# A transformer layer's gates' stage: landing buffers of their own for the mixing of the second FFN matrix, and weights asked for two ahead

## The chip, the cores and the metric

One core of a Trainium2 chip runs the whole kernel as one program. The metric is the device time of one execution in microseconds (us); lower is better. Engines are named as the profile names them: PE (TensorE matmul), PEld (its weight loads), DVE (VectorE), ACT (ScalarE), POOL (GpSimd), and SP (SyncE), which here only issues DMAs.

## The reference, cut to what matters

One layer of an encoder: sequence 1024, width 1024, float32. Attention outputs `o_a` (512 wide) and `o_b` (256 wide) are each projected to 1024, weighed by two sigmoid gates of the layer's input, added, projected once more, and followed by a SwiGLU FFN of width 2816.

```python
gate_a, gate_b = jnp.split(jax.nn.sigmoid(gates + b_gate[l]), 2, axis=-1)
merged = gate_a * (o_a @ w_proj_a[l]) + gate_b * (o_b @ w_proj_b[l])
x = x + gt1 * (merged @ w_o[l])

h2 = rms_norm(x, g_norm2[l]) * (1.0 + sc2) + sh2
a, up = jnp.split(h2 @ w_ffn_in[l], 2, axis=-1)
x = x + gt2 * ((jax.nn.silu(a) * up) @ w_ffn_out[l])
```

The second FFN product `@ w_ffn_out` is done at the end of the kernel as a two-by-two block product with seven block multiplications in place of eight; this needs four sums and differences ("mixings") of the blocks of `w_ffn_out`, which are made much earlier, in the stage that this case is about.

## The kernel before, in words

Every float32 operand of a large product is split into a high part (rounded, made by ACT) and a low part (the difference, made by POOL or DVE), and each product takes three matmul passes: high by high, high by low, low by high. A weight tile `raw` of 128x512 lands by DMA (`wload`, a ring of 6 buffers), ACT writes `whi`, and POOL writes `wlo` (`wsplit`, a ring of 10 pairs).

The stages, in order of the program: input projections and attention; the **gates' stage** (PE multiplies the layer's input `hT` with gate weights `in_wg`, ACT takes the sigmoid out of PSUM into `sg`); the **merges** (PE multiplies `oT`, the attention outputs, with `in_wpa` and `in_wpb`; DVE multiplies with the gates and adds; ACT and DVE split the sum into `h2T`); the **wo stage** (the product with `w_o`, token tile by token tile); the FFN's first and second products.

In the gates' stage PE does 21 halves of 24 matmuls each, 128x512: one for the gate (2, 1), then two for each of (3, 0), (3, 1), up to (7, 1). Banks of PSUM for them come in pairs, two of `d` for branch 0 and two of `s` for branch 1, so a half can begin when the sigmoid four halves earlier in this alternation (two halves earlier in its own branch's pair) has been read out. Meanwhile, off PE, two other things are done:

- `o_split`: twelve 128x512 pieces of the attention outputs are read back from `o_d` in DRAM and split into the two tiles `oT0` and `oT1`, which the merges multiply with.
- `w2_combos(k)` for k = 0 to 10: four blocks of `w_ffn_out` (called `in_w` in the profile, as are all weights of the FFN) are loaded, POOL and DVE make two differences each, in place, and four results are stored to `w2_d` (`w_d` in the profile).

The merges are `merge(i)` for i in `MORD` = 3, 4, 5, 6, 7, 2, 0, 1. Beside them `w_o` is brought in: `wo_keep` puts five of its eight row blocks into tiles `wr` that replace gates no longer needed, `wo_slot` puts three into the ring of pairs. `KFIRST` is the order in which the first token tile of the wo stage takes these eight.

PE's order is that of the code. On ACT, DVE, POOL and SP a planner orders the instructions of this part of the program, each engine then runs its list strictly in order, and an instruction that waits holds all behind it on its engine. All DMAs here are issued by SP, and eight counters are used in turn for their ends, so that a DMA is issued only when the eighth before it has landed. Space in SBUF is a stack at each side; a pool that is opened where another was closed waits, tile by tile, for the last use of what lay there.

Of the kernel before, what the change touches and what calls it, by code (L numbers as in the profile page):

```python
# [10 lines left out]
F32 = mybir.dt.float32  # L11
F32R = mybir.dt.float32r
# [3 lines left out]
S = 1024  # L16
# [4 lines left out]
HT = 11  # L21
# [4 lines left out]
LATE = (3, 4, 5, 6, 7)  # L26
MORD = (3, 4, 5, 6, 7, 2, 0, 1)
MSIG = {0: ((2, 0), (2, 1)), 1: ((0, 0), (0, 1)), 2: ((1, 0), (1, 1))}
MKEEP = {3: 3, 4: 4, 5: 5, 6: 6, 7: 7}
MSLOT = {5: 2, 6: 0, 7: 1}  # L30
KFIRST, KLAST, OT = (3, 4, 5, 2, 6, 0, 7, 1), (2, 0, 1, 3, 4, 5, 6, 7), 3
PP, QT, AQ, AT, AV = 100, 0, 0, 0, 0
WARM = 40
XSQ = "avavaaaa"
# [5 lines left out]
def hybrid_layer(ctx: ExitStack, tc: tile.TileContext, x, colp, wada1, wada2, bada2, wqkv, wg, wpa, wpb,  # L40
                 wo, w1, w2, hgain, ropeg, rope, rbias, bmask, g2r, out):
    nc = tc.nc

    def pool(name, side, **kw):
        return tc.alloc_tile_pool(name=name, bufs=1, side=side, reuse_waits="tile", **kw)
# [16 lines left out]
    def bank(tag):  # L62
        return ps.tile([128, 512], F32, tag=tag, name="ps_" + tag)
# [26 lines left out]
    def fview(ap):  # L90
        return ap.bitcast(F32)

    def wload(src, n):
        raw = wp.tile([128, 512], F32, tag="raw", bufs=NRAW, name="raw")
        nc.sync.dma_start(raw[:, :n], src)
        return raw[:, :n]

    def wsplit(r, eng=None):
        n = r.shape[1]
        hi = wp.tile([128, 512], F32R, tag="hi", bufs=NHL, name="whi")  # L100
        lo = wp.tile([128, 512], F32R, tag="lo", bufs=NHL, name="wlo")
        nc.scalar.activation(hi[:, :n], r, AF.Copy)  # L102
        (eng or nc.gpsimd).tensor_sub(lo[:, :n], r, fview(hi[:, :n]))  # L103
        return hi, lo

    def wslot(src, n):
        return wsplit(wload(src, n))
# [27 lines left out]
    def big(name, shape=None, dtype=F32):  # L135
        return ap_.tile(shape or wide, dtype, tag="big", bufs=NBIG, name=name)

    yT = [ap_.tile([128, 4, S], F32, tag="qk", bufs=2, name="yT") for _ in range(2)]
    land = [big("land") for _ in range(NBIG)]
# [433 lines left out]
    def mm_set(pb, wsl, src, ksrc, n, ntot, done, hs):  # L573
        for j in range(n):
            for i, (a, b) in enumerate(PASS):
                nc.tensor.matmul(pb, wsl[a][:, j * 128:(j + 1) * 128], src[b][:, ksrc + j, hs],  # L576
                                 start=(done == 0 and j == 0 and i == 0),
                                 stop=(done + j == ntot - 1 and i == 2))
# [3 lines left out]
    def gate_w(i, br):  # L582
        if (i, br) not in gw:
            gw[i, br] = [wslot(wg[i, :, 8 * br + 4 * j:8 * br + 4 * j + 4, :], 512) for j in range(2)]
# [230 lines left out]
    def sig_tile(i, br):  # L815
        z = sgp.tile(wide, F32, tag="sg", bufs=10, name="sg")
        for hf in range(2):
            sig.setdefault((i, br, hf), z[:, hf * 512:hf * 512 + 512])
# [2 lines left out]
        for br in range(2):  # L821
            sig_tile(i, br)
    sig[2, 1, 1] = sgp.tile([128, 512], F32, name="s2")
    op_ = pool("o", "right")
    oT = [op_.tile([128, 6, S], F32R, name=f"oT{i}") for i in range(2)]

    def gates(i, br):
        gate_w(i, br)
        for hf in range(2):
            hs = slice(hf * 512, hf * 512 + 512)  # L830
            if i * 4 + br * 2 + hf < NPRE:
                continue
            pb = bank("ds"[br])
            for j in range(2):
                mm_set(pb, gw[i, br][j], hT, 4 * j, 4, 8, 4 * j, hs)
            nc.scalar.activation(sig[i, br, hf], pb, AF.Sigmoid, bias=bg_c[:, 8 * br + i:8 * br + i + 1])  # L836

    def sig_load(i, br, hf):
        if i * 4 + br * 2 + hf < NPRE:
            hs = slice(hf * 512, hf * 512 + 512)  # L840
            nc.sync.dma_start(sig[i, br, hf], sig_d[i, br][:, hs])
            nc.scalar.activation(sig[i, br, hf], sig[i, br, hf], AF.Sigmoid)
# [3 lines left out]
    def merge_w(i):  # L846
        if i not in mw:
            mw[i] = wslot(wpa[i], 512), wslot(wpb[i], 256)

    def merge(i):  # L850
        merge_w(i)
        wa, wb = mw[i]
        for hf in range(2):
            hs = slice(hf * 512, hf * 512 + 512)
            ppa, ppb = bank("tv"[hf]), bank("ds"[hf])
            mm_set(ppa, wa, oT, 0, 4, 4, 0, hs)
            mm_set(ppb, wb, oT, 4, 2, 2, 0, hs)
            m, sb = sig[i, 0, hf], sig[i, 1, hf]
            nc.vector.tensor_mul(m, m, ppa)
            nc.vector.tensor_mul(sb, sb, ppb)  # L860
            nc.vector.tensor_add(m, m, sb)
            nc.scalar.activation(h2T[0][:, i, hs], m, AF.Copy)
            nc.vector.tensor_sub(h2T[1][:, i, hs], m, fview(h2T[0][:, i, hs]))

    def o_split():
        for pr in (4, 5, 0, 1, 2, 3):
            for hf in range(2):
                hs = slice(hf * 512, hf * 512 + 512)
                raw = wp.tile([128, 512], F32, tag="raw", bufs=NRAW, name="raw")
                nc.sync.dma_start(raw, o_d[pr][:, hs])  # L870
                hi, lo = oT[0][:, pr, hs], oT[1][:, pr, hs]
                if pr < 4:
                    hi, lo = (z[:, pr].rearrange("p (r w) -> p w r", r=16)[:, 32 * hf:32 * hf + 32] for z in oT)
                    raw = raw.rearrange("p (w r) -> p w r", r=16)
                nc.scalar.activation(hi, raw, AF.Copy)
                (nc.gpsimd if hf else nc.vector).tensor_sub(lo, raw, fview(hi))

    def w2_combos(k):
        b = {}
        for r in range(2):  # L880
            for c in range(2):
                b[r, c] = wload(w2[(k + HT * r) * 128:(k + HT * r + 1) * 128, c * 512:c * 512 + 512], 512)
        t1, t3, t2, t4 = b[0, 0], b[0, 1], b[1, 1], b[1, 0]
        nc.gpsimd.tensor_sub(t1, b[0, 1], b[0, 0])
        nc.vector.tensor_sub(t3, b[1, 1], b[0, 1])
        nc.gpsimd.tensor_sub(t2, b[1, 1], t1)
        nc.vector.tensor_sub(t4, b[1, 0], t2)
        for n, z in enumerate((t1, t2, t3, t4)):
            nc.sync.dma_start(w2_d[n, k], z)

    wow = {}

    def wo_raw(hf, k):
        return wload(wo[k * 128:(k + 1) * 128, hf * 512:hf * 512 + 512], 512)

    def wo_keep(k):

        hi, lo = (sgp.tile(wide, F32R, tag="sg", bufs=10, name="wr") for _ in range(2))
        for hf in range(2):
            hs = slice(hf * 512, hf * 512 + 512)  # L900
            raw = wo_raw(hf, k)
            nc.scalar.activation(hi[:, hs], raw, AF.Copy)
            nc.gpsimd.tensor_sub(lo[:, hs], raw, fview(hi[:, hs]))
            wow[hf, k] = hi[:, hs], lo[:, hs]

    def wo_slot(k):
        for hf in range(2):
            wow[hf, k] = wsplit(wo_raw(hf, k))

    gates(2, 1)  # L910
    n = 0
    for i in LATE:
        for br in range(2):
            gates(i, br)
            if i == 3 and br == 0:
                o_split()
            else:
                w2_combos(n)
                n += 1
    h1l.release()  # L920
    h1p.release()
    h2p = pool("h2", "left")
    h2T = [h2p.tile([128, KT, S], F32R, name=f"h2T{i}") for i in range(2)]

    for n, i in enumerate(MORD):
        merge(i)
        if n == 0:
            w2_combos(9)
            w2_combos(10)
        for z in MSIG.get(n, ()):  # L930
            sig_tile(*z)
            for hf in range(2):
                sig_load(*z, hf)
        if n in MSLOT:
            wo_slot(MSLOT[n])
        if n + 1 < 8:
            merge_w(MORD[n + 1])
        if n in MKEEP:
            wo_keep(MKEEP[n])
    op_.release()  # L940
# [390 lines left out]
```

## Time and profile before

| | us |
|---|---|
| median of 3 runs | 1605.3 (1605.08 to 1607.59) |
| the profiled execution | 1608.76, of which the span of the trace 1607.0 |
| gates' stage and merges, in the span | 635.5 to 832.9 |
| PE busy | 1547.5 (96% of the span) |
| DVE, POOL, ACT busy | 996.6, 694.9, 650.5 |

Times of the trace count from the start of the span. "Busy" for PE has the modelled ends of pipelined matmuls in it, so a 96% busy PE may still lose time; how many matmuls start in a stretch says more. In rows that list instructions, "x" is a count, and what stands in square brackets is the idle time of the engine before it and what ended it. In the table of stretches each engine has its busy time and the number of its instructions, then come the clock that PE was granted (1.00 is full), the mean busy share of the 16 DMA engines, and GB/s.

### The profile page before, as it was taken

How to read it: one execution, taken by the hardware profiler on the slowest of the kernel's cores; microseconds unless marked ns; L12 is line 12 of the kernel's file. 1: busy time of each engine (PE TensorE's matmuls, PEld its weight loads, DVE VectorE, ACT ScalarE, POOL GpSimd, SP SyncE). 2: the span in 40 equal slices, each digit the busy share in tenths (PEclk: the TensorE clock that was granted, in tenths of full speed). 3: DMA queues.
4: the chain of work that ended last, by engine and by line, in shares of the span. 5: the costliest groups of instructions: out<-in, count | busy, mean ns of one | idle time of the engine just before them, and what ended most of it. 6: DMA issues, size and time to landing. Idle time of an engine off the chain costs nothing.

```text
span 1607.0 us, 24545 instructions
## 1 busy us (share of the span) xinstructions
PE 1547.5 (96%) x8240; PEld 1292.7 (80%) x8240; DVE 996.6 (62%) x2162; ACT 650.5 (40%) x1694; POOL 694.9 (43%) x658
## 2 busy tenths in 40 slices
PE   8999999999999999998999996999999999999998
PEld 7888888898888877876778875788888888888886
DVE  6766676766988743322474559866666666435476
ACT  5555555555645453311442223323333333344442
POOL 1432232221101041554362246876676666545566
PEclk9999999999999999999999998999999999999999
DMA  8332231344244352777534111333333333576775
GB/s 338 102 102 78 85 115 47 122 127 133 84 132 129 94 168 68 231 251 243 164 120 178 66 46 40 102 115 105 100 109 100 105 98 120 192 218 193 246 218 171
DMA packets 144446, 219.11 MB, mean 136 GB/s; under 512 B 26800, under 2 KB 64560, under 8 KB 144320
## 3 DMA queue, kind: packets, MB, share of 16 engines
q1 hardware_dynamic: 144320, 217.55, 42.3%
q8 instruction: 65, 1.06, 0.3%
q14 instruction: 61, 0.50, 0.1%
HBM read 163.90 MB, written 53.59 MB: 135 GB/s over the span
## 4 chain that ended last, share of the span: by engine, by line
PE 73%; DVE 9%; DMA 8%; POOL 3%; issue 3%; ACT 3%; SPq 0%; POOLq 0%; DVEq 0%; ACTq 0%
PE ps_d L287 13%; PE ps_t L1071 6%; PE ps_s L1071 6%; PE ps_v L1071 6%; PE ps_d L1071 6%; PE ps_d L598 4%; PE ps_d L1173 3%; PE ps_s L1173 3%; DMA raw<-in_w_dram 2%; PE ps_d L993 2%; PE ps_v L1173 2%; PE ps_t L1173 2%; PE ps_v L576 2%; PE ps_s L438 2%; PE ps_v L479 2%
## 5 line engine op out<-in xcount | busy, mean ns | idle before, releaser
L103 POOL TENSOR_TENSOR wlo<-raw,whi 128x512 fp32r<-128x512 f32 (+2 forms) x245 | 327.3, 1343 | 415.4 <-ACT whi L102 411.0
L102 ACT ACTIVATE whi<-raw 128x512 fp32r<-128x512 f32 (+1 forms) x376 | 218.2, 602 | 382.0 <-DMA raw<-in_wg_dram 71.5
L287 PE MATMUL ps_d<-whi,hT 128*128 128x384 f32 x1152 | 317.1, 343 | 0.5 <-ACT v L322 0.5
L287 PEld LDWEIGHTS ps_d<-whi,hT 128*128 128x128 f32 x1152 | 210.1, 188 | 6.2 <-ACT vs L325 3.5
L103 DVE TENSOR_TENSOR wlo<-raw,whi 128x512 fp32r<-128x512 f32 (+1 forms) x131 | 130.8, 1008 | 103.8 <-ACT whi L102 94.7
L287 PE MATMUL ps_d<-wlo,hT 128*128 128x384 f32 x576 | 193.6, 336 | 0.9 <-POOL wlo L103 0.7
L287 PEld LDWEIGHTS ps_d<-wlo,hT 128*128 128x128 f32 x576 | 108.5, 188 | 1.5 <-POOL wlo L103 1.5
L317 POOL TENSOR_TENSOR ra<-qn,rtab 128x64 f32<-128x64 f32 x48 | 17.1, 357 | 165.8 <-DVE qn L310 125.3
L102 ACT ACTIVATE whi<-ws 128x512 fp32r<-128x512 f32 x60 | 37.9, 632 | 117.0 <-DVE ws L1081 32.1
L1008 POOL TENSOR_TENSOR c<-c 128x512 f32<-128x512 f32 x40 | 63.5, 1588 | 50.2 <-DVE c L1121 42.6
L453 ACT ACTIVATE P<-P,st 128x256 f32<-128x256 f32 (+2 forms) x100 | 46.2, 464 | 69.2 <-DVE st L452 69.1
L1071 PE MATMUL ps_t<-t,whi 128*128 128x512 f32 x160 | 52.0, 406 | 14.4 <-DVE c L1007 12.8
L308 DVE TENSOR_REDUCE ss<-sq 128x4 f32<-128x256 f32 x80 | 33.3, 416 | 45.6 <-ACT sq L305 45.5
L576 PE MATMUL ps_s<-hT,whi 128*128 128x512 f32 x176 | 56.5, 403 | 3.7 <-ACT sg L836 3.7
L453 ACT ACTIVATE P<-P,sx 128x384 f32<-128x384 f32 (+1 forms) x64 | 37.1, 580 | 52.8 <-DVE sx L452 52.8
L464 PE MATMUL ps_t<-ident,P 128*128 128x128 f32 (+1 forms) x336 | 51.8, 275 | 4.7 <-DVE P L456 2.0
L479 PE MATMUL ps_v<-PT,v 128*64 128x128 f32 (+1 forms) x672 | 54.7, 284 | 1.4 <-DVE PT L468 1.4
L598 PE MATMUL ps_d<-hT,whi 128*128 128x512 f32 x176 | 55.5, 397 | 0.0
L1007 DVE TENSOR_TENSOR c<-c 128x512 f32<-128x512 f32 x40 | 46.7, 1169 | 13.9 <-ACT c L1006 13.9
L438 PE MATMUL ps_s<-qk 64*128 64x256 f32 (+3 forms) x492 | 53.7, 321 | 1.6 <-DVE st L452 1.4
L438 PEld LDWEIGHTS ps_s<-qk 64*128 64x128 f32 (+1 forms) x492 | 35.0, 182 | 23.4 <-issue 12.2
L1071 PE MATMUL ps_s<-t,whi 128*128 128x512 f32 x168 | 52.9, 396 | 0.0
(377 smaller groups left out, 3972.8 us busy)
## 6 DMA issues: line engine op xcount, KB each, us to landing
raw<-in_w_dram SPq DMA_DIRECT2D x165, 256.0 KB
ga_d<-c SPq DMA_DIRECT2D x77, 256.0 KB
raw<-ga_d SPq DMA_DIRECT2D x77, 256.0 KB
wa<-in_wada_dram SPq DMA_DIRECT2D x32, 512.0 KB
raw<-in_wqkv_dram SPq DMA_DIRECT2D x80, 192.0 KB
w_d<-raw SPq DMA_DIRECT2D x44, 256.0 KB
raw<-w_d SPq DMA_DIRECT2D x44, 256.0 KB
xt<-in_x_dram SPq DMA_DIRECT2D x16, 512.0 KB
```

Source lines behind the costliest of these rows:

```text
L102: nc.scalar.activation(hi[:, :n], r, AF.Copy)
L103: (eng or nc.gpsimd).tensor_sub(lo[:, :n], r, fview(hi[:, :n]))
L287: nc.tensor.matmul(pd[:, :384], tok(a, k, t), U.w[k][b][:, :384], start=(k == 0 and i == 0), stop=(k == KT - 1 and i == 2))
L438: nc.tensor.matmul(I.pS[h][:nq, :nk], U.qk[a][hs, I.q0:I.q0 + nq], U.qk[2 + b][hs, I.kb0 * 128:I.kb0 * 128 + nk], start=(i == 0), stop=(i ...
L453: nc.scalar.activation(P[:nq, :nk], P[:nq, :nk], AF.Exp, scale=-1.0, bias=nm, accum_out=sm)
L464: nc.tensor.transpose(pt[:, i * 128:i * 128 + nq], P[:nq, i * 128:(i + 1) * 128], ident[:nq, :nq])
L479: nc.tensor.matmul(po[hs, :nq], U.v[:, I.kb0 + i, hs], I.PT[h][:, i, :nq], start=(i == 0), stop=(i == nkb - 1))
L576: nc.tensor.matmul(pb, wsl[a][:, j * 128:(j + 1) * 128], src[b][:, ksrc + j, hs], start=(done == 0 and j == 0 and i == 0), stop=(done + j ...
L598: nc.tensor.matmul(st["p"], gw[i, br][j][a][:, kk * 128:(kk + 1) * 128], hT[b][:, k, hs], start=(k == 0 and q == 0), stop=(k == 7 and q == 2))
L1008: nc.gpsimd.tensor_mul(sg, sg, up) if j not in (0, HT) else nc.vector.tensor_mul(sg, sg, up)
L1071: nc.tensor.matmul(pb, w[p][:, k * 128:(k + 1) * 128], b[q][:, k], start=(k == 0 and i == 0), stop=(k == 3 and i == 2))
L1173: nc.tensor.matmul(pb[m], o[0][a][:, m * 128:(m + 1) * 128], o[1][b], start=(k == 0 and i == 0), stop=(k == HT - 1 and i == 2))
```

## The change: what it does

- `w2_combos` no longer takes its loads from the ring `raw`. It has 22 landing buffers of its own (`l`, 2 KB in each partition), in a pool `land` that lies where `oT` lay and is closed before `oT` is opened.
- So `o_split` moves from the start of the gates' stage to behind the ninth gate (6, 1), and `oT` takes the place of the landing buffers.
- All eleven mixings are spread over the first nine gates (a table `W2C`); two of them stood in the merges before.
- The weights of a gate are asked for two gates ahead, those of a merge two merges ahead.
- `wo_slot` stands one merge earlier each time, with its second half's `wlo` on DVE, and `KFIRST` is reordered to match.

```diff
-MSLOT = {5: 2, 6: 0, 7: 1}
+MSLOT = {4: 2, 5: 0, 6: 1}
+NLAND = 22
+W2C = {0: (0,), 1: (1,), 2: (2, 3), 3: (4,), 4: (5,), 5: (6, 7), 6: (8,), 7: (9,), 8: (10,)}
-KFIRST, KLAST, OT = (3, 4, 5, 2, 6, 0, 7, 1), (2, 0, 1, 3, 4, 5, 6, 7), 3
+KFIRST, KLAST, OT = (3, 4, 2, 0, 5, 6, 1, 7), (2, 0, 1, 3, 4, 5, 6, 7), 3
...
-    op_ = pool("o", "right")
-    oT = [op_.tile([128, 6, S], F32R, name=f"oT{i}") for i in range(2)]
+    lnd = pool("land", "right")
...
-                b[r, c] = wload(w2[(k + HT * r) * 128:(k + HT * r + 1) * 128, c * 512:c * 512 + 512], 512)
+                b[r, c] = lnd.tile([128, 512], F32, tag="l", bufs=NLAND, name="l")
+                nc.sync.dma_start(b[r, c], w2[(k + HT * r) * 128:(k + HT * r + 1) * 128, c * 512:c * 512 + 512])
...
-            wow[hf, k] = wsplit(wo_raw(hf, k))
-
-    gates(2, 1)
-    n = 0
-    for i in LATE:
-        for br in range(2):
-            gates(i, br)
-            if i == 3 and br == 0:
-                o_split()
-            else:
-                w2_combos(n)
-                n += 1
+            wow[hf, k] = wsplit(wo_raw(hf, k), nc.vector if hf else None)
+
+    GS = [(2, 1)] + [(i, br) for i in LATE for br in range(2)]
+    for n, z in enumerate(GS):
+        for y in GS[n:n + 3]:
+            gate_w(*y)
+        gates(*z)
+        for k in W2C.get(n, ()):
+            w2_combos(k)
+        if n == max(W2C):
+            lnd.release()
+            op_ = pool("o", "right")
+            oT = [op_.tile([128, 6, S], F32R, name=f"oT{i}") for i in range(2)]
+            o_split()
...
     for n, i in enumerate(MORD):
+        for z in MORD[n:n + 2]:
+            merge_w(z)
         merge(i)
-        if n == 0:
-            w2_combos(9)
-            w2_combos(10)
...
+        if n + 2 < 8:
+            merge_w(MORD[n + 2])
         if n in MSLOT:
             wo_slot(MSLOT[n])
-        if n + 1 < 8:
-            merge_w(MORD[n + 1])
```

What the planner makes of it is seen in the engines' lists. SP's list before, where the gates' stage begins (`o_d<-stg` and `sig_d<-gsig` are the last stores of the attention stage):

```order
L483 DMA o_d<-stg 128x128
L870 DMA raw<-o_d 128x512 x6
L95 DMA raw<-in_w_dram 128x512 x4
L95 DMA raw<-in_wg_dram 128x512 x2
L889 DMA w_d<-raw 128x512 x2
L95 DMA raw<-in_w_dram 128x512 x2
L889 DMA w_d<-raw 128x512
```

SP's list of the changed kernel at the same place:

```order
L97 DMA raw<-in_wg_dram 128x512
L485 DMA o_d<-stg 128x128
L607 DMA sig_d<-gsig 128x512
L485 DMA o_d<-stg 128x128
L884 DMA l<-in_w_dram 128x512 x9
L891 DMA w_d<-l 128x512
L884 DMA l<-in_w_dram 128x512
L891 DMA w_d<-l 128x512
L884 DMA l<-in_w_dram 128x512 x2
L891 DMA w_d<-l 128x512 x3
```

Nine loads of the second FFN matrix now stand ahead of the first store of a mixing, and no gate weight stands among them: ten of the sixteen loads of gate weights that stood in this stage have moved ahead of it, into the attention stage's part of the list.

SP's list of the changed kernel where the mixings end:

```order
L884 DMA l<-in_w_dram 128x512 x2
L871 DMA raw<-o_d 128x512
L891 DMA w_d<-l 128x512 x3
L871 DMA raw<-o_d 128x512
L891 DMA w_d<-l 128x512
L871 DMA raw<-o_d 128x512
L891 DMA w_d<-l 128x512 x7
L871 DMA raw<-o_d 128x512 x6
L97 DMA raw<-in_wpa_dram 128x512
L97 DMA raw<-in_wpb_dram 128x256
```

The reading back of `o_d`, which stood first in the stage, now surrounds the last stores of the mixings, with the weights of the first merge behind it.

ACT's list before, at the start of the gates' stage (`oT` is the high part of the attention outputs, `sg` and `s` are sigmoids):

```order
L604 ACTIVATE gsig<-ps_d,cp 128x512
L875 ACTIVATE oT_9080<-raw 128x512 x4
L875 ACTIVATE oT_9080<-raw 128x32x16 x2
L836 ACT_TABLE_LOAD
L836 ACTIVATE s_9076<-ps_s,cp 128x512
L875 ACTIVATE oT_9080<-raw 128x32x16 x6
L836 ACTIVATE sg<-ps_d,cp 128x512
```

ACT's list of the changed kernel, from the fourteenth sigmoid of the gates' stage on:

```order
L837 ACTIVATE sg<-ps_d,cp 128x512
L876 ACTIVATE oT_9798<-raw 128x512 x4
L876 ACTIVATE oT_9798<-raw 128x32x16 x2
L837 ACTIVATE sg<-ps_d,cp 128x512
L876 ACTIVATE oT_9798<-raw 128x32x16 x5
L837 ACTIVATE sg<-ps_s,cp 128x512
L876 ACTIVATE oT_9798<-raw 128x32x16
L104 ACTIVATE whi<-raw 128x512
L104 ACTIVATE whi<-raw 128x256
```

The twelve activations into `oT` have moved from ahead of the first sigmoids to between the fourteenth and the seventeenth; the first of them waits for the last stores of the eleven mixings, since `oT` lies in their buffers. Two more merges' weights (`whi`, four rows) follow before the seventeenth sigmoid.

## The prediction

> **What bounds the kernel now.** I read the page's first part for the span, then the stretches of the stage, PE's list of instructions in order of time, and then the lists of the engines that PE waits for. The page:
>
> ```profile
> span 1607.0 us, 24545 instructions
> ```
>
> The stretches (columns: time, then busy time and count of PE, PEld, DVE, ACT and POOL, PE's clock, DMA share, GB/s), first the gates' stage, then the merges, then four pieces:
>
> ```profile
> 635.00:758.00 123.00, 117.76 (x512) 96.31 (x512) 35.08 (x28) 33.43 (x51) 65.13 (x46) 0.97 0.72 239
> 758.00:833.00 75.00, 70.81 (x292) 56.58 (x291) 43.92 (x56) 30.06 (x55) 33.80 (x28) 0.95 0.44 143
> 8.00:12.00 4.00, 3.37 (x31) 3.13 (x30) 2.37 (x8) 2.44 (x7) 0.00 (x0) 1.00 1.03 409
> 659.00:667.00 8.00, 8.00 (x37) 6.60 (x37) 1.61 (x3) 0.64 (x2) 2.97 (x4) 1.00 0.85 284
> 723.00:731.00 8.00, 4.31 (x14) 3.14 (x14) 2.44 (x2) 2.30 (x4) 4.56 (x4) 0.75 0.77 268
> ```
>
> PE is the only engine near full, yet between 723 and 731 it started 14 matmuls where it had started 37 between 659 and 667, at a clock of 0.75. PE's own list gives the pace and the holes:
>
> ```profile
> 635.54 0.74 PE L576 MATMUL ps_s<-hT,whi 128*128 128x512 f32 x2
> ...
> 708.14 0.73 PE L576 MATMUL ps_d<-hT,whi 128*128 128x512 f32 x2 [1.55 <-ACT sg L836]
> ...
> 720.77 0.62 PE L576 MATMUL ps_s<-hT,whi 128*128 128x512 f32 x2
> 721.22 0.39 PE L576 MATMUL ps_s<-hT,wlo 128*128 128x512 f32 x1
> 721.45 0.61 PE L576 MATMUL ps_s<-hT,whi 128*128 128x512 f32 x2
> ...
> 728.70 1.22 PE L576 MATMUL ps_s<-hT,whi 128*128 128x512 f32 x2 [3.69 <-ACT sg L836]
> ...
> 758.42 0.63 PE L576 MATMUL ps_t<-oT,whi 128*128 128x512 f32 x2
> ...
> 765.57 1.22 PE L576 MATMUL ps_d<-oT,whi 128*128 128x512 f32 x2 [4.19 <-ACT sg L836]
> ...
> 832.94 0.87 PE L993 MATMUL ps_d<-wr,h2T 128*128 128x512 f32 x3
> 836.99 6.51 PE L993 MATMUL ps_d<-wr,h2T 128*128 128x512 f32 x15 [3.18 <-DVE sg L860]
> ```
>
> The stage's first matmul starts at 635.54, that of the merges at 758.42, that of the wo stage at 832.94. Undisturbed, three matmuls take 721.45 - 720.77 = 0.68 us, so a half of 24 takes 8 x 0.68 = 5.44 us and the 21 halves 114.2: the gates could end at 749.8 and end at 758.4, 8.6 us late. The merges' undisturbed pace stands in the chain of waits, twelve matmuls in 2.81 us:
>
> ```profile
> 774.06 2.81 PE ps_t L576 x12
> ```
>
> Their 288 matmuls (eight merges, six blocks, two halves, three passes) need 67.5 us and take 74.5, 7.0 late. All of it sits at three holes, 1.55, 3.69 and 4.19 us = 9.4 together; the other 6.2 are mostly matmuls at half clock behind the two longer ones (1.22 us for a pair at 728.70 against 0.62 at 720.77).
>
> All three holes end on a sigmoid `sg`. ACT's list shows what kept it:
>
> ```profile
> 696.84 1.29 ACT L102 ACTIVATE whi<-raw 128x512 fp32r<-128x512 f32 x2 [8.86 <-DMA raw<-in_wg_dram]
> 698.03 0.67 ACT L836 ACTIVATE sg<-ps_s,cp 128x512 f32<-128x512 f32 x1
> ...
> 717.38 1.26 ACT L102 ACTIVATE whi<-raw 128x512 fp32r<-128x512 f32 x2 [8.19 <-DMA raw<-in_wg_dram]
> 718.55 0.67 ACT L836 ACTIVATE sg<-ps_s,cp 128x512 f32<-128x512 f32 x1
> ...
> 727.45 0.63 ACT L102 ACTIVATE whi<-raw 128x512 fp32r<-128x512 f32 x1 [8.23 <-DMA raw<-in_wg_dram]
> 727.98 0.67 ACT L836 ACTIVATE sg<-ps_s,cp 128x512 f32<-128x512 f32 x1
> ```
>
> ACT stands idle 8 to 9 us before a gate weight that has not landed, with sigmoids behind it. The weight is late because SP's list is held. Its waits in 635 to 760, the four of the stores L889:
>
> ```profile
> SPq L889 <- POOL raw L884: 27.1, 10, 4.0
> SPq L889 <- POOL raw L886: 10.5, 11, 1.0
> SPq L889 <- DVE raw L885: 10.2, 11, 2.8
> SPq L889 <- DVE raw L887: 9.3, 10, 1.0
> ```
>
> SP waits 57 us of 125 for mixings whose stores are next in its list, and four of the ring's six buffers hold one mixing, so the next weight cannot be asked for. The DMA share meanwhile is 0.72.
>
> **The change part by part.** *Weights two ahead, and buffers of their own.* Ten of the sixteen gate loads now come before the stage; of the other six the last stands 62nd among its transfers, so at some 0.85 us each (below) lands near 691. It serves the sixteenth half, due at 635.5 + 15 x 5.44 = 717.1: 26 us of cover. The three holes then go, 15.6 us, if nothing takes their place.
>
> *The mixings, squeezed into nine gates.* What is late next is `oT`. All its activations on ACT wait for the last store of a mixing, at a time I call T, and three sigmoids, the 15th to 17th, stand behind them. T is a sum of transfers of 256 KB: 44 loads, 44 stores, 6 gate weights and 6 of the `o_d` loads, 100, behind one another since only eight are in flight. The start comes from SP's list, the latency from the chain:
>
> ```profile
> 636.18 0.38 SPq L483 DMA_DIRECT2D o_d<-stg  x1
> ```
> ```profile
> 660.22 1.91 DMA raw<-in_w_dram
> ```
>
> So the first lands near 636.6 + 1.9 = 638.5 and T = 638.5 + 99 p, where p is the time of one transfer. No row shows these 100 without SP's waits. Bounds: the stage's 239 GB/s at a share of 0.72 make 332 at a full share, p = 262144 B / 332 = 0.79 us, T = 716.7; the 284 GB/s of 659:667 as it stands make 0.92, T = 729.9. Further out, the 409 GB/s of 8:12, reads only, make 0.64, T = 702, and the unchanged 239 make 1.10, T = 747. I take 0.85, between the two nearest: SP's waits shrink but stay in the list. T = 722.7.
>
> DMA and not the engines should set T. The mixing's four operations, and the two for `oT`:
>
> ```profile
> L884 POOL TENSOR_TENSOR raw<-raw x11: 1261/1287/1295, 652.1 to 749.5; 128x512 f32<-128x512 f32 x11
> ```
> ```profile
> L885 DVE TENSOR_TENSOR raw<-raw x11: 691/693/694, 654.0 to 756.2; 128x512 f32<-128x512 f32 x11
> ```
> ```profile
> L886 POOL TENSOR_TENSOR raw<-raw x11: 1262/1292/1297, 656.7 to 757.0; 128x512 f32<-128x512 f32 x11
> ```
> ```profile
> L887 DVE TENSOR_TENSOR raw<-raw x11: 1752/1762/1772, 658.0 to 758.3; 128x512 f32<-128x512 f32 x11
> ```
> ```profile
> L875 ACT ACTIVATE oT<-raw x12: 619/1132/1364, 635.6 to 648.8; 128x512 fp32r<-128x512 f32 x12
> ```
> ```profile
> L876 POOL TENSOR_TENSOR oT<-raw,oT x6: 1303/1924/2528, 636.9 to 650.0; 128x512 fp32r<-128x512 f32 x6
> ```
>
> One after the other they are 1.29 + 0.69 + 1.29 + 1.76 = 5.03 us a mixing, 55.3 for eleven, against 84 us of transfers. POOL has 22 x 1.29 = 28.4 of them and some eleven low parts of weights, differences of the same size and so at the same 1.29, 14, in the same 84.
>
> *What hangs on T.* Behind T come, on the path to the 17th sigmoid: one activation 0.6, six low parts on POOL at 1.92 = 11.5 (the ring's six buffers must come free before the second six can land), about 3 for that second landing, 2.3 for the merges' four weights on ACT (two of 128x512 take 1.29, the other two are half as wide), 0.4 for the last activation, 0.7 for the sigmoid: T + 18.5. The 21st half needs it, at 635.5 + 20 x 5.44 = 744.3. So T may be as late as 725.8 (p = 0.88, 297 GB/s) at no cost, and each us beyond is a us lost. The 15th and 16th sigmoids (T + 5.5 by 733.4, T + 11.8 by 738.9) and the first merge (T + 17 by 749.8) allow more. At 722.7 the margin is 3.1 us: nothing lost.
>
> *Merges and `wo_slot`.* Two mixings leave this stage, eight loads and eight stores at a share of 0.44, so its weights come sooner. Three low parts of 128x512 go from POOL to DVE, about 1 us each by the 0.69 to 1.76 above, under 75 - 43.9 = 31 us of idle DVE. `KFIRST` has the same eight blocks. The first token tile's hole at 836.99 hangs on the last merge's DVE work, which stays: 0, with -6 (hole and half clock gone: 15 matmuls in 6.51 us against 3.4) and +3 (a second such hole) as bounds.
>
> Sum: -8.6 - 7.0 + 0 = -15.6. The profiled execution took 1608.76 (span 1607.0 and 1.76 around it) and would become 1593.2; it lies 3.5 above the median of 1605.3, from which I take the saving: **1589.7**.
>
> **The rivals.** *A: the last store is late.* If p lies between 0.88 and 1.0, the sigmoids behind `oT` open a new hole at the 19th to 21st half. At 0.92, T = 729.9, 4.1 us too late, and a hole like that of 3.69 us brought half clock, worth (3.18-us hole, 6.51 - 3.4) 3.1: the time is 1605.3 - 15.6 + 7.2 = 1596.9; at 1.0 (T = 737.5) 1604.5. For it: no stretch shown moved more than 284 GB/s with loads and stores mixed. Against it: SP waited in every one of them. The Trainium skill, "TensorE: Matmul & The Clock Gate", Part 1, says that the clock halves after about one idle window of some 3.4 us; by it a lateness of 4.1 us dealt to three holes costs no half clock, and A's time would be about 3 us less. The trace agrees as far as the hole of 1.55 us was followed by a pair at 0.73 us; that 3.18 us sufficed shows that the figure is no sharp edge. On p, the Trainium skill, "HBM Reference", Specifications (TRN2), gives about 358 GB/s as a core's share and some 425 for a core alone; an estimate from 358 is T = 711, 15 us ahead of need, which speaks against A. The 409 of 8:12 agree for reads; no row here shows it for stores.
>
> *B: slower than before.* The list's own waits, not the buffers, set the pace: stores wait for POOL in SP's order as before, and 100 transfers go at 239 GB/s. T = 747.1, 21.3 late, with half clock 24.4: 1614.1. It decides from a lateness of 15.6 - 3.1 = 12.5, T = 738.3, p = 1.01 (260 GB/s). For it: the stage never ran far above that pace. Against it: those 57 us of waits came with four loads ahead of their mixing; now nine stand ahead of the first store.
>
> *C: the change does not do what it says.* The sigmoids wait for something that no weight ends, and the holes stay: 1605.3. Against it: three rows of ACT name the weight's DMA, each with a sigmoid close behind.
>
> **How the numbers follow.** My forecast (no hole, p below 0.88) has 0.62, since its bound of 0.88 lies above the middle of the two nearest prices but below the worse; A 0.26, B 0.06, C 0.06. The time of the likeliest is 1589.7. The range reaches down to 1585 (most of the transition's -6) and up to 1600 (A at p = 0.95: T = 732.6, 6.8 late, +9.9), which leaves out B, C and A's slow end, some 0.17. A measurement of this kernel tells about 0.2%, 3.2 us, from no change. Faster by more: the forecast and nearly all of A, 0.86; within: C and A's end, 0.08; slower: B, 0.06. The forecast's own range is 1585 to 1593.
>
> **What the profile after should show.** No hole on `sg` in PE's list before 750, merges starting near 750 and the wo stage near 817; no ACT wait of 8 us on `in_wg`; a DMA share over 0.85 and over 290 GB/s from 640 to T; the last `w_d` store landing at 719 to 726; ACT's first `oT` row right behind it. A is seen as a hole before the 19th to 21st half with ACT's `oT` rows ahead of the sigmoid; B as that hole over 12 us long with SP still waiting on POOL. I would be wrong if a resource that I held hidden carries the end: POOL in the mixings, SP's order between the stores and the `o_d` loads, or the weights of the first merges behind them.

## The result and the profile after

| | before | changed |
|---|---|---|
| median of 4 runs (us) | 1606.44 (1605.08 to 1609.12) | 1589.15 (1587.58 to 1590.5) |
| the profiled execution, its span | 1608.76, 1607.0 | 1587.91, 1586.1 |

The ratio is 0.989 (95% interval 0.9871 to 0.9909): 17.7 us faster, between 14.6 and 20.7. The forecast was 15.6 us faster. Chips differ by some us in the kernel before (medians of 1601.6 to 1607.9 in the experiments below), so kernels are compared by their ratios to the kernel before that ran beside them.

In the changed kernel's chain of waits PE follows on PE from the gates' stage into the wo stage, with no other engine between them:

```profile
637.69 5.71 PE ps_s L578 x24
643.39 10.88 PE ps_d L578 x48
...
741.31 10.88 PE ps_s L578 x48
752.19 2.81 PE ps_t L578 x12
...
818.26 1.41 PE ps_s L578 x6
819.66 11.16 PE ps_d L996 x48
```

Two halves take 10.88 us from the second on, exactly twice 5.44. The stage lasts 114.5 us (637.69 to 752.19) where it lasted 122.9, the merges 67.5 where they lasted 74.5. Among PE's waits there is no row on `sg` in these stages.

The stretches of the changed kernel (columns as before):

```profile
640.00:660.00 20.00, 20.00 (x89) 16.53 (x89) 8.99 (x7) 5.97 (x9) 14.83 (x11) 1.00 0.97 358
660.00:680.00 20.00, 20.00 (x90) 16.56 (x89) 11.80 (x10) 4.86 (x8) 15.65 (x12) 1.00 1.03 383
700.00:704.00 4.00, 4.00 (x20) 3.30 (x19) 2.36 (x2) 0.69 (x1) 2.77 (x4) 1.00 1.06 405
712.00:716.00 4.00, 4.00 (x20) 3.30 (x19) 0.61 (x1) 1.85 (x4) 0.04 (x1) 1.00 0.00 0
```

The DMA engines are full (0.97 to 1.06, 358 to 405 GB/s in these stretches) until the stores are through, and then stand still. SP's list and its longest waits:

```profile
638.74 4.32 SPq L884 DMA_DIRECT2D l<-in_w_dram  x9
...
702.22 4.18 SPq L891 DMA_DIRECT2D w_d<-l  x7
716.11 6.77 SPq L871 DMA_DIRECT2D raw<-o_d  x6
```
```profile
SPq L97 <- POOL wlo L105: 20.1, 10, 8.5
SPq L871 <- DVE oT L877: 13.8, 4, 9.5
...
SPq L891 <- POOL l L886: 1.6, 2, 1.4
SPq L891 <- DVE l L889: 1.3, 2, 1.1
```

Stores hardly wait for mixings any more: the four rows that held SP for 57 us before come to 4 together (L887 has 0.9, L888 0.3). The longest waits that are left are those of loads (L97 for weights, L871 for `o_d`) for a buffer of their ring, and no store is among them. ACT's list at the place that the prediction worried about:

```profile
714.15 0.69 ACT L837 ACTIVATE sg<-ps_d,cp 128x512 f32<-128x512 f32 x1 [4.75 <-PE ps_d L578]
714.74 4.17 ACT L876 ACTIVATE oT<-raw 128x512 fp32r<-128x512 f32 x6
719.59 0.69 ACT L837 ACTIVATE sg<-ps_d,cp 128x512 f32<-128x512 f32 x1 [0.69 <-PE ps_d L578]
720.18 5.13 ACT L876 ACTIVATE oT<-raw 128x512 fp32r<-128x512 f32 x5
...
731.88 0.67 ACT L837 ACTIVATE sg<-ps_s,cp 128x512 f32<-128x512 f32 x1
```

The first `oT` row follows the fourteenth sigmoid at once, which itself waited for PE; it did not wait for a store. T was near 710 (the last of seven stores issued by 706.4, no traffic from 712 to 716).

### The profile page after: what moved, and what is told of

Read it like the earlier page. It is cut to its first block, busy times and chain, and to the rows that moved or that the text cites. A ratio compares the mean times of both kernels' runs of the same rounds, so it can differ in the third digit from the quotient of the medians.

```text
span 1586.1 us, 24543 instructions
## 1 busy us (share of the span) xinstructions
PE 1538.9 (97%) x8240; PEld 1287.4 (81%) x8240; DVE 998.7 (63%) x2165; ACT 652.0 (41%) x1694; POOL 689.0 (43%) x655
## 3 DMA queue, kind: packets, MB, share of 16 engines
q8 instruction: 65, 1.06, 0.3%
## 4 chain that ended last, share of the span: by engine, by line
PE 81%; DVE 9%; DMA 4%; issue 2%; ACT 2%; POOL 1%; SPq 0%; POOLq 0%; DVEq 0%; ACTq 0%
PE ps_d L289 14%; PE ps_t L1074 6%; PE ps_s L1074 6%; PE ps_v L1074 6%; PE ps_d L1074 6%; PE ps_s L578 5%; PE ps_d L578 4%; PE ps_d L600 4%; PE ps_s L1176 3%; PE ps_d L1176 3%; PE ps_v L1176 2%; PE ps_t L1176 2%; PE ps_v L481 2%; PE ps_s L440 2%; PE ps_v L578 2%
## 5 line engine op out<-in xcount | busy, mean ns | idle before, releaser
L105 POOL TENSOR_TENSOR wlo<-raw,whi 128x512 fp32r<-128x512 f32 (+2 forms) x242 | 319.8, 1328 | 472.7 <-ACT whi L104 438.6
L105 DVE TENSOR_TENSOR wlo<-raw,whi 128x512 fp32r<-128x512 f32 (+1 forms) x134 | 134.5, 1014 | 103.6 <-ACT whi L104 95.8
L455 ACT ACTIVATE P<-P,st 128x256 f32<-128x256 f32 (+2 forms) x100 | 46.2, 463 | 69.4 <-DVE st L454 69.3
```

Source lines behind the costliest of these rows:

```text
L455: nc.scalar.activation(P[:nq, :nk], P[:nq, :nk], AF.Exp, scale=-1.0, bias=nm, accum_out=sm)
```

## The experiments

**Which part brings the gain.** Four kernels ran together, each against the kernel before.

*The changed kernel with the w_o part taken back:*

```diff
-MSLOT = {4: 2, 5: 0, 6: 1}
+MSLOT = {5: 2, 6: 0, 7: 1}
...
-KFIRST, KLAST, OT = (3, 4, 2, 0, 5, 6, 1, 7), (2, 0, 1, 3, 4, 5, 6, 7), 3
+KFIRST, KLAST, OT = (3, 4, 5, 2, 6, 0, 7, 1), (2, 0, 1, 3, 4, 5, 6, 7), 3
...
-            wow[hf, k] = wsplit(wo_raw(hf, k), nc.vector if hf else None)
+            wow[hf, k] = wsplit(wo_raw(hf, k))
```

> The changed kernel with the w_o part taken back (wo_slot at merges 5, 6, 7 of the order, its second half's wlo on POOL, the old KFIRST). Theory S (the hole of 3.2 us at the first token tile before was made by wo_slot's late place: its weights wait for ring pairs that the last merge frees, and hold ACT's last activations): the hole of 3 us and the half clock behind it come back, about 6 us slower than the changed kernel, 1595. Rival R (the hole was a consequence of the merges' late weights and sigmoids, and went with them): no hole, within 2 us of the changed kernel, 1589.

Measured 1588.98, ratio 0.9888 (0.987 to 0.9906), the same as the changed kernel. Its first token tile has no hole. Theory S fell here: the w_o part isn't needed for the gain.

*The kernel before with the w_o part alone* (the same lines the other way round):

> The kernel before with the w_o part of the change alone. Theory S: the hole at the first token tile goes, the gates' stage and the merges stay as they were: about 6 us faster than before, 1600. Rival R: nothing moves, within 2 us of 1606.

Measured 1603.87, ratio 0.9977 (0.9963 to 0.999): 1.6 to 5.9 us faster, less than the 6 or so that theory S said. The gates' and merges' holes stay, but PE's wait of 3.2 us at the first token tile is 0.2. So rival R fell as well: the hole can go by either part.

*The changed kernel with weights asked for as before:*

```diff
-        for y in GS[n:n + 3]:
-            gate_w(*y)
...
-        for z in MORD[n:n + 2]:
-            merge_w(z)
         merge(i)
...
-        if n + 2 < 8:
-            merge_w(MORD[n + 2])
         if n in MSLOT:
             wo_slot(MSLOT[n])
+        if n + 1 < 8:
+            merge_w(MORD[n + 1])
```

> The changed kernel with weights asked for as before (a gate's where the gate is written, a merge's one ahead), landing buffers kept. Theory L (the ring shared with the mixings held the weights; buffers of their own are what matters): gates in 114 to 117 us, at most 3 us slower than the changed kernel, 1589 to 1592; what it may lose is at the last two gates, whose four loads now stand behind all stores and the reading back of o_d. Rival W (asking earlier is what matters): the holes on sigmoids come back, 8 to 15 us slower, 1597 to 1604.

Measured 1589.56, ratio 0.9891 (0.9874 to 0.9909): theory L. Its gates take 114.4 us. Asking two ahead adds nothing once the mixings have left the ring; the planner already puts the loads early where the ring lets it: two of the gates' loads stand in the stage here, six in the changed kernel.

*The kernel before with weights two ahead, mixings in the shared ring* (the same asking written into its loops):

> The kernel before with weights of gates and merges asked for two ahead, the mixings still in the shared ring. Theory L: SP still waits over 40 us for mixings with stores at the head of its list, and the merges' weights stand behind the last mixings: a gain of at most half, 0 to 8 us, 1598 to 1606. Rival W: gates back to back in 114 to 116 us and merges in under 70, 13 to 16 us faster, 1590 to 1593.

Measured 1600.77, ratio 0.9965 (0.9951 to 0.9979): theory L again, a third of the gain. Its merges run at full pace (761.48 to 828.95, 67.5 us), its gates don't: they take 125.0 us, 2.1 more than before. ACT's rows and PE's:

```profile
737.85 0.94 ACT L102 ACTIVATE whi<-raw 128x512 fp32r<-128x512 f32 x2 [24.18 <-DMA raw<-in_wpa_dram]
742.02 0.63 ACT L102 ACTIVATE whi<-raw 128x512 fp32r<-128x512 f32 x1 [3.24 <-DMA raw<-in_wpa_dram]
```
```profile
743.28 1.22 PE L576 MATMUL ps_d<-hT,whi 128*128 128x512 f32 x2 [8.59 <-ACT sg L836]
```

The early rows stand on ACT ahead of sigmoids that were ready, and the weights that they wait for sit behind mixings in SP's list: one hole of 8.59 us instead of three. The hole at the first token tile is small here too (waits of 0.5 and 0.3 us), so part of this kernel's gain is that hole and not the weights.

**Buffers or order.** *The changed kernel without landing buffers*, `o_split` still late:

```diff
-    lnd = pool("land", "right")
+    op_ = pool("o", "right")
+    oT = [op_.tile([128, 6, S], F32R, name=f"oT{i}") for i in range(2)]
...
-                b[r, c] = lnd.tile([128, 512], F32, tag="l", bufs=NLAND, name="l")
-                nc.sync.dma_start(b[r, c], w2[...])
+                b[r, c] = wload(w2[...], 512)
...
```

> The changed kernel without landing buffers: the mixings' loads go through the weights' ring again, while o_split stays behind the ninth gate, oT has its place from the start, and weights are asked for two ahead. Theory L (apart buffers keep the weights from waiting on mixings): SP waits over 40 us with stores at the head of its list, PE gets holes on sigmoids again, 1597 to 1610. Rival O (the late o_split and the order of the mixings bring the gain, not the buffers): no hole, 1588 to 1592.

Measured 1600.5 against 1601.57 of the kernel before beside it, ratio 0.9991 (0.998 to 1.0002): theory L, the gain is gone. Two kernels with landing buffers that also ran beside it, with 6 buffers and with 22 stores added (both below), took 1587.74 and 1587.36, some 13 us less. SP waits for mixings again (38.8 us with the three other rows, a little under the 40 expected) and ACT for what stands behind them:

```profile
SPq L891 <- POOL raw L886: 22.0, 7, 4.8
```
```profile
706.42 0.63 ACT L104 ACTIVATE whi<-raw 128x512 fp32r<-128x512 f32 x1 [8.54 <-DMA raw<-in_wg_dram]
...
717.82 0.63 ACT L877 ACTIVATE oT<-raw 128x512 fp32r<-128x512 f32 x1 [7.94 <-DMA raw<-o_d]
```
```profile
719.08 1.22 PE L578 MATMUL ps_d<-hT,whi 128*128 128x512 f32 x2 [6.82 <-ACT sg L838]
...
734.51 0.73 PE L578 MATMUL ps_s<-hT,whi 128*128 128x512 f32 x2 [1.95 <-ACT sg L838]
```

In this profile the gates take 126.0 us (761.85 - 635.81) where the changed kernel's take 114.4, while the merges run at full pace (67.5 us) and the first token tile has no hole. So what the buffers pay is paid in the gates' stage; the merges' pace and the first token tile come without them.

The converse, own buffers with `oT` in its place from the start, has no place in SBUF: beside `oT` there is no room for them. So the late `o_split` is what makes room for the buffers, and the buffers are what pays. One rival stays open. With landing buffers there are also more buffers in all, and no run here gives the shared ring more of them; whether that would do as well is not shown.

**How many buffers.** The changed kernel with one number changed (8 and 4 ran together, 6 on another chip):

```diff
-NLAND = 22
+NLAND = 8
```

> The changed kernel with 8 landing buffers in place of 22. The theory (buffers apart from the weights' ring are what matters; their number only sets how far the last store stands ahead of its need): no hole on a sigmoid in the gates' stage, SP waits again for mixings, the last store lands 5 to 20 us later than 709 and so still before the 726 to 730 it may, within 2 us of the changed kernel: 1588 to 1591. Rival (22 buffers are needed): last store after 735, 8 us slower or more, from 1597.

> The changed kernel with 6 landing buffers. With 8 the last store landed near 724 and cost nothing, with 4 near 757 and the merges started 18 us late. If the end of the mixings moves evenly with the number, the last store lands between 735 and 745, and the merges, 12 to 17 us behind it, start 0 to 8 us late: 1588 to 1598. Rival (two whole mixings in flight are what is needed, 8 buffers): as with 4, from 1603.

> The changed kernel with 4 landing buffers, one mixing at a time, the pace of the kernel before (10 us a mixing) in buffers that are still apart from the weights. The theory: weights never late, no hole in the gates before the 21st half, but the last store lands near 745 to 758, and the first merge, 17 us behind it, starts at 762 to 775 in place of 752: 10 to 26 us with the half clock, 1600 to 1615. Rival (the margin behind the last store is much larger than 17 us said, or the pace was set by the shared ring): 1588 to 1592.

| buffers | last stores issued until | merges start, us after the gates' first matmul (PE's rows) | ratio |
|---|---|---|---|
| 22 | 706.4 | 114.4 | 0.9890 (0.9871 to 0.9909) |
| 8 | 721.6 | 114.4 | 0.9871 (0.9857 to 0.9886) |
| 6 | about 731 | 117.3 | 0.9911 (0.9887 to 0.9935) |
| 4 | 754.6 | 132.7 | 1.0021 (1.0006 to 1.0036) |

Eight are as good as 22, though SP's stores wait for mixings again, 21.7 us in all: the last store still comes early enough. With six the profile has one hole of 2.6 us on a sigmoid; the ratio alone does not tell six from 22. With four the whole gain is lost, though PE waits for no sigmoid: the hole has moved to the first merge. Its rows, SP's wait, ACT and PE:

```profile
SPq L891 <- POOL l L886: 25.3, 11, 3.7
```
```profile
760.88 1.07 ACT L876 ACTIVATE oT<-raw 128x512 fp32r<-128x512 f32 x1 [25.42 <-DMA raw<-o_d]
```
```profile
769.14 1.22 PE L578 MATMUL ps_t<-oT,whi 128*128 128x512 f32 x2 [18.09 <-ACT whi L104]
```

The last six loads of `o_d` stand behind the last stores in SP's list (758.33), the stores behind the mixings, and `oT` behind them. This is close to the prediction's rival B, with its signs (SP waiting on POOL, a hole over 12 us) and nearly its time (1610.06 against 1614.1), but with the hole at the first merge and not before a sigmoid.

**How much slack there is.** The changed kernel with stores made again into a DRAM tile `w2_e` that nothing reads (`w_e` in the profile). With 22 added, two of each mixing's four stores are made twice; with 44 all four are, which is the edit shown; with 66 two of the four are made a third time. The planner lists them with the rest:

```diff
...
             nc.sync.dma_start(w2_d[n, k], z)
+            if n < 4:
+                nc.sync.dma_start(w2_e[n, k], z)
```

> The changed kernel with 22 more stores (two of each mixing's four made twice). The theory: T = 709.4 + 22 x 0.70 = 725, no hole, within 2 us of the changed kernel, 1587 to 1591: the transfers up to this point are hidden. Rival (no free margin: each transfer in the stage costs): 22 x 0.5 = 11 us more as between 44 and 66, 1600.

> The changed kernel with every store of a mixing made twice, the second into a DRAM tile that nothing reads: 44 transfers more. The theory (T is a sum of transfers of 0.70 us each and the first merge needs T + 15 to 17): T = 709.4 + 44 x 0.70 = 740, first merge at 755 to 757 in place of 752, 3 to 8 us slower with half clock, 1592 to 1598. Rival (SP's waits or the engines set T, so that transfers are free): within 2 us of the changed kernel, 1589.

> The same with 66 transfers more. The theory: T = 709.4 + 66 x 0.70 = 756, first merge at 770 to 773, 18 to 24 us slower with half clock, 1607 to 1613; against the kernel with 44 a slope of 0.7 us for each transfer. Rival (transfers free): 1589.

| stores added | gates' first matmul | first merge | PE's wait there | ratio |
|---|---|---|---|---|
| 22 | 634.02 | 748.43 | none | 0.9914 (0.9891 to 0.9936) |
| 44 | 635.35 | 757.05 | 7.13 and 2.0 | 0.9945 (0.993 to 0.996) |
| 66 | 635.51 | 766.84 | 16.75 and 2.1 | 1.0018 (1.0009 to 1.0028) |

With 22 the profile has no hole and the stages last 114.4 and 67.5 us as without; its ratio lies some 4 us above the changed kernel's 0.989, but the two intervals overlap, so the time alone does not tell. With 44 the time was 1599.52, 1.5 us over the range that was expected, with 66 it was 1610.8, inside its range. The first merge starts where it was said with 44 (757.05), and 3 us ahead of that with 66. The slope between the two is 0.51 us for each transfer and not 0.7. ACT's and PE's rows with 66:

```profile
754.80 5.11 ACT L877 ACTIVATE oT<-raw 128x512 fp32r<-128x512 f32 x7 [3.99 <-DMA w_e<-l]
```
```profile
766.84 1.22 PE L579 MATMUL ps_t<-oT,whi 128*128 128x512 f32 x2 [16.75 <-ACT whi L105]
```

Here T is seen directly: `oT` starts when the last `w_e` store lands, 754.8, which is 119.3 us into the stage. In the changed kernel T was 710 - 637.6 = 72.4 into it. The 66 transfers cost 46.9 us, 0.71 each; transfers do set T. The first merge follows T by 12.0 us. From 44 to 66 its start moved 9.6 us and not 22 x 0.70 = 15, which is why the slope fell short: with 44 the planner had put `oT` behind the nineteenth sigmoid, so that ACT reached it at 745.11, when the stores were already through.

**The hole at the first token tile.** *The kernel before with one line of the w_o part:*

```diff
-MSLOT = {5: 2, 6: 0, 7: 1}
+MSLOT = {4: 2, 5: 0, 6: 1}
```

> The kernel before with one line of the w_o part, wo_slot one merge earlier each time; the old KFIRST, and all low parts on POOL. Theory S' (the hole of 3.2 us at the first token tile came from ACT's list, where the last slot's whi rows stood between the last merges' h2T activations and waited for ring pairs that PE still held): no hole there, holes of gates and merges as before, 2 to 6 us faster than before, 1600 to 1605. Rival (the low part moved to DVE, or KFIRST, took the hole away in the kernel with all three): hole of about 3 us as before, within 2 us of 1606.

Measured 1604.19, ratio 0.9982 (0.9968 to 0.9995): 0.8 to 5.1 us faster, theory S'; `KFIRST` and DVE's low parts are not needed for it. Its other holes stay (2.39, 2.57 and 4.40 us). ACT and DVE at the end of the merges in the kernel before, then ACT and PE here:

```profile
833.21 0.63 ACT L102 ACTIVATE whi<-raw 128x512 fp32r<-128x512 f32 x1 [1.14 <-PE ps_s L576]
833.75 0.61 ACT L862 ACTIVATE h2T<-sg 128x512 fp32r<-128x512 f32 x1
```
```profile
834.39 1.34 DVE L863 TENSOR_TENSOR h2T<-sg,h2T 128x512 fp32r<-128x512 f32 x1 [2.18 <-ACT h2T L862]
```
```profile
830.50 0.63 ACT L102 ACTIVATE whi<-raw 128x512 fp32r<-128x512 f32 x1 [0.99 <-DMA raw<-in_w_dram]
831.04 0.62 ACT L862 ACTIVATE h2T<-sg 128x512 fp32r<-128x512 f32 x1
```
```profile
834.01 4.38 PE L993 MATMUL ps_d<-wr,h2T 128*128 128x512 f32 x18
```

Before, a `whi` row waited for a ring pair that PE's merges still read, and the `h2T` row behind it came 0.8 us after the wo stage's first matmul; here it comes 3.0 us ahead of it. DVE's strict list hung on it (the wait of 2.18 us), and on DVE's next rows the PSUM bank that PE wanted. In the changed kernel with the old `MSLOT` the `h2T` row comes 3.3 us ahead (813.38 against 816.70): the planner wrote the end of ACT's list in the good order by itself, which is why two different parts cure it.

## Why the prediction was right, point by point

| term | forecast | measured |
|---|---|---|
| gates' stage | 122.9 to 114.2 us | 114.5 |
| merges | 74.5 to 67.5 us | 67.5 |
| first token tile | 0 (-6 to +3) | -6.2 in the two profiles |
| time of one transfer, p | 0.85 us | 0.70 |
| T, the last store | 722.7 | 710 |
| T to the first merge | 17 us | 12.0 (with 66 stores added) |

The two stages' terms, the pace of undisturbed PE less what it took, held within 0.3 us. The cause was one of the two named together: buffers apart from the ring (0.989 with them, 0.9991 without). The other, weights two ahead, turned out not to be needed (0.9891 without it).

One reading was inexact. Of the three rows of ACT that the prediction shows, only the one at 727.45 stands ahead of a hole of PE. The holes at 708.14 and 765.57 hang on these rows of the kernel before:

```profile
706.88 0.63 ACT L102 ACTIVATE whi<-raw 128x512 fp32r<-128x512 f32 x1 [8.18 <-DMA raw<-in_wg_dram]
...
757.41 0.94 ACT L102 ACTIVATE whi<-raw 128x512 fp32r<-128x512 f32 x2 [16.91 <-DMA raw<-in_wpa_dram]
762.45 0.63 ACT L102 ACTIVATE whi<-raw 128x512 fp32r<-128x512 f32 x1 [4.10 <-DMA raw<-in_wpa_dram]
...
764.85 0.67 ACT L836 ACTIVATE sg<-ps_d,cp 128x512 f32<-128x512 f32 x1
```

So the longest hole, 4.19 us, waited for the weights of merges and not of a gate. The mechanism is the same, a late weight ahead of a ready sigmoid.

The term that was mis-sized is the transition. It was set to 0 on the ground that the last merge's DVE work stays; what mattered was a `whi` row ahead of that work on ACT, and the order at the end of ACT's list was not compared. Eighteen matmuls of the first token tile took 843.34 - 832.94 = 10.4 us before and about 4.2 after. In time over several runs the hole is worth less, 3 to 4 us by the kernels that remove it alone (ratios 0.9982 and 0.9977). Forecast and hole together make 15.6 + 3 to 4 = 19; the ratio's interval, 14.6 to 20.7, holds it. That the time itself came within 0.6 us of the forecast's 1589.7 is partly luck: the saving was larger by 1.7 us in the medians, and the kernel before was 1.1 us slower in the four runs than in the three that the forecast started from.

p was too careful, and so was the distance from T to the merges. Both errors made the margin look smaller than it was, and cost the number nothing. The bound of 332 GB/s, the stage's traffic put to a full share, was itself too low: 69.3 us from the first landing (638.74 + 1.9 = 640.6) to 710 for 99 transfers are 0.70 us, 374 GB/s. T fell 16 us ahead of the 725.8 allowed, 18 if the stage's later start is counted. The estimate of T from the page "HBM Reference", Specifications (TRN2), of the Trainium skill, 711, was nearer than the one from the trace's slices; the core read and wrote 374 GB/s here, between that page's 358 as a core's share and its 425 for a core alone.

What should be seen in the profile was seen but for two points: the last store landed near 710 and not at 719 to 726, and `oT` did not follow it but the fourteenth sigmoid, 4 us behind T. No hole on `sg`, merges at 752 (start 637.7, so 114.5 later; 750 was said for a start at 635.5), share over 0.85.

The two profiles differ by 20.9 us in span: 8.4 gates, 7.0 merges, 6.2 first token tile, less 2.1 since the stage began later, and 1.4 elsewhere. The medians differ by 17.3, as the profile of before was 2.3 above its median and that of after 1.2 below. The later start isn't the change's: the gates' first matmul lies between 634.0 and 640.0 in the profiles of the experiments' twelve kernels, and at 634.8 in the kernel with the w_o part taken back, whose SP list is the same row for row up to there.

## What to carry to other kernels

When a queue issues loads and stores in one list, a store that waits for an engine holds every load behind it; buffers of their own for the stored data cured that here, asking earlier into the same ring did not. Price a stage's transfers between two bounds, its own traffic put to a full share and the fastest stretch of the trace (332 and 409 GB/s here, and 374 came of it), and then ask with doubled transfers or fewer buffers how far the margin reaches: here 8 buffers did what 22 do, and 4 gave everything back. When a change moves rows on an in-order engine, compare the end of each list too, not only the place that the change is about.

## What the runs showed of the hardware that was not expected

Loads and stores mixed ran at 405 GB/s and a DMA share of 1.05 to 1.06 for 8 us (700 to 708), as fast as the reads alone at the kernel's start (409).

The half clock behind a hole of PE does not go by the hole's length alone. Rows of PE's list with what follows: the kernel before with the earlier slots, the same, and the kernel with 6 landing buffers.

```profile
709.80 0.73 PE L576 MATMUL ps_d<-hT,whi 128*128 128x512 f32 x2 [2.39 <-ACT sg L836]
...
711.82 1.05 PE L576 MATMUL ps_d<-hT,whi 128*128 128x512 f32 x2
```
```profile
730.60 0.79 PE L576 MATMUL ps_s<-hT,whi 128*128 128x512 f32 x2 [2.57 <-ACT sg L836]
731.19 0.63 PE L576 MATMUL ps_s<-hT,wlo 128*128 128x512 f32 x1
731.62 1.05 PE L576 MATMUL ps_s<-hT,whi 128*128 128x512 f32 x2
```
```profile
747.65 0.73 PE L578 MATMUL ps_s<-hT,whi 128*128 128x512 f32 x2 [2.63 <-ACT sg L837]
748.22 0.39 PE L578 MATMUL ps_s<-hT,wlo 128*128 128x512 f32 x1
748.45 0.62 PE L578 MATMUL ps_s<-hT,whi 128*128 128x512 f32 x2
```

Holes of 2.39 and 2.57 us brought pairs of 1.05 us one or two pairs later, the hole of 2.63 us brought none (0.62). The prediction had no row between its hole of 1.55 us, which cost no clock, and that of 3.18, which did. The Trainium skill, "TensorE: Matmul & The Clock Gate", Part 1, has the clock halve after at least one idle window of some 3.4 us, and has this window run freely. These rows differ from the first: holes of 2.39 and 2.57 us are shorter than such a window and cost the clock all the same. A window that runs freely would fit them, as the hole's place in it would then count and not the length alone, but no run here shows that this is the reason.
